# Gate k-steps between the attention's and the last heads' dependent matmuls, and x transposed earlier

## The chip, the cores and the metric

The program runs on one core of one Trainium2 chip. The metric is device time in microseconds of one launch, as the median of several runs; lower is better.

## The reference

One layer of a decoder trunk with eight sampled sequences of one new token each (NS = 8) beside one prompt of 1024 tokens (NP = 1024, NT = NP + NS = 1032 columns), at a model width of 1024, in float32:

```python
h  = rmsnorm(x) * (1 + scale1) + shift1              # shift, scale, gate from the conditioning c
z  = h @ w_in                                        # q|k|v, output gate, beta, decay, swa q|k|v, ga, gb
y_a = gated_rmsnorm(gated_delta_rule(conv4(q, k, v))) @ w_gdn_out       # 8 heads of 128 x 128
y_b = sliding_window_attention_with_sinks(q, k, v) @ w_swa_out          # 16 q heads, 4 kv heads, window 128
x  = x + gate1 * ((sigmoid(ga) * y_a + sigmoid(gb) * y_b) @ w_o)
h2 = rmsnorm(x) * (1 + scale2) + shift2
x  = x + gate2 * ((silu(dwconv3(h2 @ w_ffn_gate)) * (h2 @ w_ffn_up)) @ w_ffn_down)
return rmsnorm(x), and the new states (delta matrix, conv rows, window k and v, ffn conv rows)
```

## The kernel before

Activations lie transposed, features on partitions. A projection takes one column tile of 128 columns of `w_in` and runs over 8 slices of the contraction (k-steps) and three parts of the columns (384, 384 and 264 wide). Each k-step is a triple of matmuls, since an operand is split in a high and a low half: `mm3` (L168, L169, L170) adds high by high, low by high and high by low. The weights of a tile come by one transfer into a `raw` buffer (L132) and are split by ScalarE (L126) and VectorE (L127).

The stages of the first half are, in order: conditioning and modulation; `attention` of the prompt, four kv groups of 8 blocks, with the sampled sequences' own attention (`sample_softmax`) queued ahead of the last group's first block; eight DeltaNet heads; `branches` (the two output projections, and the sampled sequences' delta step). The FFN is the second half.

An attention block makes score products (L561, L562), a softmax on VectorE and ScalarE, transposes of the result (`pt`, L178) and value products (L598, L600).

A head runs five generators at once, which `weave` queues under different priorities. `unit_inverse` inverts a triangular matrix per chunk in rounds (matmuls L959 to L995). `head_projections` first projects this head's output gate (`sg`, one buffer, which is free again once the scan of the head before has read it for the last time at L904), and then q, k and v of head h + 2. `delta_scan` goes through the 8 chunks one after another: in each, L870, L873 and L877 depend on one another, with a VectorE or ScalarE step between them. `delta_prepare` makes head h + 1 ready: K and Q transposed back (`tp`, L178), their squares on ScalarE (L817), then K by K and Q by K (L835, L836), from which the next inverse starts.

`gates()` (L1186) is filler: 16 column tiles (the two branch gates, 8 tiles each), 16 x 3 x 8 = 384 k-steps, handed out one step at a time. A part ends with a tanh on ScalarE (L1198), an affine step on GpSimd and a store (L1200). Each tile's weights go into the place `fill_side`, which has one buffer each for the high half, the low half and the raw rows.

The order of instructions is that of a list scheduler: among those that a model of their times holds ready, the one of lowest priority number comes next. `later(f, by)` raises the number. `issue_after(ins)` pins what is queued under it behind one instruction. Each engine then runs its instructions strictly in that order. In a head the fillers have the number 10000, behind everything:

```python
streams = [(self.unit_inverse(pool, psum, h, prep[0]), 0, 1),
           (self.head_projections(pa, pool, h), 500, 100),
           (self.delta_scan(pool, psum, h, prep), 100, 1),
           (self.pieces(3), 10000, 100)]
```

`turn_rows` (L762) transposes x, nine row tiles, for the residual of the second half, and stores it; it runs in head 6. `last_rows` (L1019) transposes the last conv rows of the sequences and runs in head 7. All projections and fillers share two PSUM banks, pmm with two buffers and pmf with one.

Of the kernel before, what the change touches and what calls it, by code (L numbers as in the profile page):

```python
# [62 lines left out]
class Step:  # L63
    def __init__(self, ctx, tc, I, O):
# [12 lines left out]
        self.filler, self.ahead, self.fill_psum = iter(()), False, self.pmf  # L77

# [82 lines left out]

# [244 lines left out]
    def attention(self, pool, psum):  # L406
# [9 lines left out]
        self.filler, self.fill_where, self.gt = self.gates(), self.where, (pool, "vch")  # L416
# [115 lines left out]
    def attention_group(self, pool, psum, g, Q, KH, KL, V, sink):  # L532

        nc = self.nc
        for n0 in (0, 4):
# [14 lines left out]
    def attention_block(self, pool, psum, g, n, Q, KH, KL, V, sink, ob):  # L550
# [211 lines left out]
    def turn_rows(self, pa, pool):  # L762

        nc, I = self.nc, self.I
        self.xT = self.t(self.dr, [KC, P, NT], "xT")
        ys = [self.t(pool, [P, NCH, P], tag) for tag in "KQ"]
        for i, c in enumerate(range(0, NT, P)):
            w = min(P, NT - c)
            x, y = self.t(pa, [P, NT + 3], "z")[:, :NP], ys[i % 2]
            src = I["x_prompt"][0][c:c + P, :] if w == P else I["x_sample"].rearrange("b s d -> (b s) d")  # L770
            nc.sync.dma_start(x[:w], src)
            for k0 in (0, 4):
# [3 lines left out]
                nc.scalar.copy(y[:, k0:k0 + 4, :w], ps[:, :, :w])  # L776
            nc.sync.dma_start(self.xT[:, :, c:c + w].rearrange("k p n -> p k n"), y[:, :, :w])
            yield

    def delta_gate(self, pa, pool, h):  # L780
# [12 lines left out]
        self.sg = sg  # L793

# [60 lines left out]
    def delta_scan(self, pool, psum, h, prep):  # L855
# [3 lines left out]
        S = None  # L859
        so = self.t(pool, [P, NCH], "so", bufs=2)  # L860
        f = self.t(pool, [P, NCH], "f", bufs=2)
        for n in range(NCH):
# [4 lines left out]
            else:  # L867
                y = self.t(pool, [P, P], "y", bufs=2)
                ks = self.t(psum, [P, P], "rc", bufs=2)
                yield nc.tensor.matmul(ks, K[:, n, :], S, start=True, stop=True)  # L870
                nc.vector.scalar_tensor_tensor(y, ks, self.ned[:, h, n:n + 1], vn[:, n, :], op0=ALU.mult, op1=ALU.add)
            sp = self.t(psum, [P, P], "rc", bufs=2)
            yield nc.tensor.matmul(sp, W[:, n, :], y, start=True, stop=True)  # L873
# [3 lines left out]
            yield nc.tensor.matmul(ds, kd[:, n, :], s, start=True, stop=True)  # L877
# [10 lines left out]
            if n % 4 == 3:  # L888
# [10 lines left out]
                nc.vector.tensor_tensor(on, ops, bc(f[:, c0:c0 + 4], 2, P), op=ALU.mult)  # L899
# [285 lines left out]
    def gates(self):  # L1185
# [4 lines left out]
        load = lambda i: self.win(tiles[i][0], where=self.fill_where)  # L1190
# [17 lines left out]
    def branches(self, pool, pool2):  # L1208
# [3 lines left out]
        self.fill_where, self.gt, self.ahead, self.fill_psum = self.where, (pool, "sgx"), True, None  # L1212
# [3 lines left out]
        next(samples)  # L1216
# [538 lines left out]
    def run(self):  # L1755
        S, nc = ExitStack, self.nc
        self.constants()
        with S() as ca:
            with S() as c:
# [13 lines left out]
                self.attention(pool, psum)  # L1773
            pg = self.pool("pg", 1, ctx=ca)
            self.fill_side = pg, 1, 1
            self.fill_where, self.gt = self.fill_side, (pg, "gt")
            with S() as c:
# [6 lines left out]
                for h in range(H):  # L1784
                    prep = self.prep
# [12 lines left out]
        self.mm = [self.pmm, self.pmm, self.pmf]  # L1798
# [45 lines left out]
```

## Time and profile before

| what | value |
|---|---|
| median of the runs (least, most) | 2210.97 us (2206.25, 2214.44) |
| the profiled execution: time, span | 2216.06 us, 2214.3 us |
| TensorE busy | 2123.2 us, 96% of the span |
| VectorE, ScalarE, GpSimd busy | 1335.3, 801.2, 303.3 us |
| data moved | 228.16 MB, 103 GB/s over the span |
| attention's last group | about 377 to 428 us |
| the eight heads | about 458 to 1174 us |

Rows of a timeline give start, duration, engine, line, operation, output and inputs, and in brackets how long the engine sat idle before it and what released it. Rows of a table of windows give the window, its length, each engine's busy time with its count of instructions, and then TensorE's granted clock, the DMA share and GB/s. "Work" below is TensorE time at the full clock; a stretch loses its length less busy time by granted clock.

### The profile page before, as it was taken

To read this page: it belongs to the slowest core of one execution; us is meant where nothing else is said; L and a number is where in the kernel's file an instruction comes from. 1 tells how busy PE (TensorE), PEld (TensorE's weight loads), DVE (VectorE), ACT (ScalarE), POOL (GpSimd) and SP (SyncE) were. 2 spreads that over 40 slices of the span, in tenths; PEclk is the share of its full clock that TensorE was granted. 3 is DMA by queue.
4 is the path that set the end of the run, shared out by engine and by line. 5 is a ranking of instruction groups with operands and counts; after the bars stand their busy time and mean duration, and the time that the engine had idled before them with its cause. 6 is when DMAs were issued, how large, how long until landed. Compare 5 with 4: busy or idle time off the path is not lost.

```text
span 2214.3 us, 41267 instructions
## 1 busy us (share of the span) xinstructions
PE 2123.2 (96%) x16573; PEld 1995.0 (90%) x16573; DVE 1335.3 (60%) x2892; ACT 801.2 (36%) x2037; POOL 303.3 (14%) x395
## 2 busy tenths in 40 slices
PE   7998999899899999999978999999999999999998
PEld 3695788699899999999968899999999999999998
DVE  4556667574474664755423565468776776866565
ACT  3445445433333334234332032344343433421102
POOL 2000000022122121121110200002332332100000
PEclk8998999799999999999988999999999999999999
DMA  9411333232232231232753663612323222253202
GB/s 340 140 40 39 115 117 106 82 79 49 73 83 69 53 91 52 65 89 73 199 140 107 206 187 99 184 61 68 108 70 96 68 94 70 96 215 129 88 3 78
DMA packets 271346, 228.16 MB, mean 103 GB/s; under 512 B 57566, under 2 KB 237697, under 8 KB 271138
## 3 DMA queue, kind: packets, MB, share of 16 engines
q1 hardware_dynamic: 269826, 221.23, 32.5%
q10 hardware_dynamic: 1152, 3.70, 0.4%
q8 instruction: 130, 2.13, 0.4%
q14 instruction: 62, 0.51, 0.1%
q0 software_dynamic: 176, 0.59, 0.1%
HBM read 175.51 MB, written 52.35 MB: 103 GB/s over the span
## 4 chain that ended last, share of the span: by engine, by line
PE 84%; DVE 6%; DMA 5%; ACT 2%; issue 1%; SPq 1%; POOL 0%; DVEq 0%; POOLq 0%; ACTq 0%
PE mm L168 19%; PE mm L169 18%; PE mm L170 18%; PE wv L168 2%; PE wv L169 2%; PE wv L170 2%; PE wy L170 2%; PE wy L168 2%; PE wy L169 2%; PE pv L600 1%; PE mm L252 1%; PE pv L598 1%; PE pt L178 1%; PE tp L178 1%; PE sc L561 1%
## 5 line engine op out<-in xcount | busy, mean ns | idle before, releaser
L168 PE MATMUL mm<-b1h,wh 128*128 128x384 f32 (+1 forms) x1440 | 476.0, 332 | 9.6 <-DVE kx L496 4.5
L170 PE MATMUL mm<-b1h,wl 128*128 128x384 f32 (+1 forms) x1440 | 469.2, 327 | 3.9 <-DVE wl L127 3.9
L169 PE MATMUL mm<-b1l,wh 128*128 128x384 f32 (+1 forms) x1440 | 468.8, 326 | 0.1
L168 PEld LDWEIGHTS mm<-b1h,wh 128*128 128x128 f32 x1440 | 274.3, 191 | 22.1 <-issue 6.3
L169 PEld LDWEIGHTS mm<-b1l,wh 128*128 128x128 f32 x1440 | 274.6, 191 | 8.6 <-issue 7.0
L170 PEld LDWEIGHTS mm<-b1h,wl 128*128 128x128 f32 x1440 | 274.0, 190 | 6.6 <-DVE wl L127 4.7
L126 ACT ACTIVATE wh<-raw 128x1024 fp32r<-128x1024 f32 x77 | 80.7, 1048 | 156.4 <-PE mm L169 103.0
L168 PE MATMUL mm<-b2h,wh 128*128 128x384 f32 (+1 forms) x384 | 123.9, 324 | 1.6 <-DVE t L1220 1.0
L168 PE MATMUL mm<-pk,w 128*128 128x260 f32 (+1 forms) x440 | 124.4, 283 | 0.9 <-ACT pk L126 0.6
L169 PE MATMUL mm<-pk,w 128*128 128x260 f32 (+1 forms) x440 | 124.2, 282 | 0.8 <-DVE pk L127 0.8
L169 PE MATMUL mm<-b2l,wh 128*128 128x384 f32 (+1 forms) x384 | 123.5, 322 | 1.2 <-DVE b2l L127 1.2
L170 PE MATMUL mm<-pk,w 128*128 128x260 f32 (+1 forms) x440 | 124.2, 282 | 0.0
L170 PE MATMUL mm<-b2h,wl 128*128 128x384 f32 (+1 forms) x384 | 122.7, 321 | 0.0
L127 DVE TENSOR_TENSOR wl<-raw,wh 128x1024 fp32r<-128x1024 f32 x76 | 93.7, 1233 | 45.6 <-ACT wh L126 44.7
L170 PE MATMUL mm<-bmh,pk 128*128 128x256 f32 (+1 forms) x380 | 108.6, 286 | 0.8 <-DVE pk L127 0.8
L168 PE MATMUL mm<-bmh,pk 128*128 128x260 f32 (+1 forms) x380 | 108.7, 286 | 0.0
L1342 DVE SCALAR_TENSOR_TENSOR x<-mm,mT,x 128x256 f32<-128x256 f32 (+2 forms) x133 | 63.4, 481 | 72.7 <-PE mm L170 70.3
L169 PE MATMUL mm<-bml,pk 128*128 128x260 f32 (+1 forms) x353 | 100.6, 285 | 0.0
L170 PE MATMUL mm<-bmh,w 128*128 128x260 f32 (+1 forms) x320 | 91.7, 287 | 0.0
L168 PE MATMUL mm<-bmh,w 128*128 128x260 f32 (+1 forms) x320 | 91.6, 286 | 0.0
L127 DVE TENSOR_TENSOR w<-ws,w 128x512 fp32r<-128x512 f32 x88 | 60.2, 685 | 41.6 <-ACT w L126 41.6
L168 PEld LDWEIGHTS mm<-pk,w 128*128 128x128 f32 x440 | 82.7, 188 | 1.5 <-ACT pk L126 0.8
(578 smaller groups left out, 5727.8 us busy)
## 6 DMA issues: line engine op xcount, KB each, us to landing
raw<-in_w_in_dram SPq DMA_DIRECT2D x60, 512.0 KB
bml<-act SPq DMA_DIRECT2D x22, 516.0 KB
raw<-in_w_ffn_gate_dram SPq DMA_DIRECT2D x22, 512.0 KB
raw<-in_w_ffn_up_dram SPq DMA_DIRECT2D x22, 512.0 KB
raw<-in_w_ffn_down_dram SPq DMA_DIRECT2D x22, 512.0 KB
qst<-in_w_mod_dram SPq DMA_DIRECT2D x16, 512.0 KB
raw<-in_w_mod_dram SPq DMA_DIRECT2D x16, 512.0 KB
act<-fa SPq DMA_DIRECT2D x22, 260.0 KB
```

The lines of the kernel that those rows point to most:

```text
L126: self.nc.scalar.activation(hi, x, AF.Copy)
L127: (eng or self.nc.vector).tensor_tensor(lo, x, hi.bitcast(F32), op=ALU.subtract)
L168: mm(ps, whi, xhi, start=first, stop=False, **kw)
L169: mm(ps, whi, xlo, start=False, stop=False, **kw)
L170: mm(ps, wlo, xhi, start=False, stop=last, **kw)
L178: self.nc.tensor.transpose(out, in_, self.ident[:p, :p])
L252: nc.tensor.matmul(ps[32 * j:32 * j + 32], self.cT[:, k0 + j, :], ws[j // 2][:, j % 2, :], start=k0 == 0, stop=k0 > 0)
L561: nc.tensor.matmul(sc[:, r, 256 - w:256], q, KH[:, lo:lo + w], start=True, stop=False)
L598: nc.tensor.matmul(out, V[:, n, ch], pc[:, r::2, :], start=True, stop=n == 0)
L600: nc.tensor.matmul(out, V[:, n - 1, ch], pp[:, r::2, :], start=False, stop=True)
L1342: nc.vector.scalar_tensor_tensor(x[:, :np_], ps[:, :np_], self.mT[:, m + j, 8:9], x[:, :np_], op0=ALU.mult, op1=ALU.add)
```

## The change

- In the attention's last group, six gate k-steps follow every block, each pinned behind the block's last score product by `issue_after` and queued at `later(..., 120)`: 8 x 6 = 48 k-steps, two column tiles.
- In heads 6 and 7 the k-steps of gates are pinned behind the scan's matmuls, two k-steps (six matmuls) behind each, by `spaced()`. Four tiles are set in each of these two heads (`pieces(12)` and `pieces(24)`). There the gate steps alternate over three PSUM buffers and two weight places.
- The low-priority filler, `pieces(3)`, is left in heads 0 to 5 alone, which leaves six tiles for it. The output gate is now a stream of its own at 500, ahead of the projections at 600.
- `turn_rows` goes from head 6 to heads 1, 2 and 3, three row tiles in each, with a store for each half of a row tile. `last_rows` goes from head 7 to head 6.
- In the scan, the transposes of the first four chunks' output are issued after chunk 5 where they were issued after chunk 3.
- In `branches`, the sampled delta step is no longer begun ahead of the loop (its first `next` is gone).

The scheduler's order on TensorE is the same up to the attention's last group and from the branches' start on; its rows number 13399 before and 13397 after. In the changed kernel line numbers are higher by 10 to 21 (L168 is L178 there, L995 is L1016, L835 is L848, and the scan's L870, L873, L877 are L889, L892, L896).

```diff
-                self.mm3(ps, whi[:, k, :], wlo[:, k, :], xh[:, k, :], xl[:, k, :], k == 0, k == KC - 1)
+                with self.spaced():
+                    self.mm3(ps, whi[:, k, :], wlo[:, k, :], xh[:, k, :], xl[:, k, :], k == 0, k == KC - 1)
+
+    def spaced(self):
+
+        if not self.steps:
+            return nullcontext()
+        self.at += 1
+        i = min(self.at // self.every, len(self.steps))
+        return self.tc.issue_after(self.steps[i - 1]) if i else nullcontext()
...
                 self.attention_block(pool, psum, g, n, Q, KH, KL, V, sink[:, 4 * g:4 * g + 4], ob)
+                if g == 3:
+                    for _ in range(6):
+                        with self.tc.issue_after(self.scored.ins):
+                            self.later(lambda: next(self.filler), 120)
             for j in range(2):
                 nc.sync.dma_start(self.ob[2 * g + j][:, n0 * P:(n0 + 4) * P], ob[:, j])
             for _ in range((2, 1, 1, 1, 2, 1, 0, 0)[2 * g + n0 // 4]):
...
-                nc.tensor.matmul(sc[:, r, 256 - w:256], q, KH[:, lo:lo + w], start=True, stop=False)
+                self.scored = nc.tensor.matmul(sc[:, r, 256 - w:256], q, KH[:, lo:lo + w], start=True, stop=False)
...

     def head_projections(self, pa, pool, h):

-        self.delta_gate(pa, pool, h)
-        yield
         if h + 2 < H:
             yield from self.delta_project(pa, pool, h + 2)
-        if h + 1 == H:
-            for _ in range(8):
-                yield from self.pieces(3)
+        else:
+            yield from self.pieces(24 if h + 1 == H else 12)

     def pieces(self, n):
...
+    def turn_rows(self, pa, i0, i1):
         nc, I = self.nc, self.I
-        self.xT = self.t(self.dr, [KC, P, NT], "xT")
-        ys = [self.t(pool, [P, NCH, P], tag) for tag in "KQ"]
-        for i, c in enumerate(range(0, NT, P)):
+        if i0 == 0:
+            self.xT = self.t(self.dr, [KC, P, NT], "xT")
+        for c in range(i0 * P, i1 * P, P):
             w = min(P, NT - c)
-            x, y = self.t(pa, [P, NT + 3], "z")[:, :NP], ys[i % 2]
+            x = self.t(pa, [P, NT + 3], "z")[:, :NP]
             src = I["x_prompt"][0][c:c + P, :] if w == P else I["x_sample"].rearrange("b s d -> (b s) d")
             nc.sync.dma_start(x[:w], src)
             for k0 in (0, 4):
                 ps = self.t(self.pmm, [P, 4, P], "mm")
                 for k in range(4):
                     self.transpose(ps[:, k, :w], x[:w, (k0 + k) * P:(k0 + k + 1) * P])
-                nc.scalar.copy(y[:, k0:k0 + 4, :w], ps[:, :, :w])
-            nc.sync.dma_start(self.xT[:, :, c:c + w].rearrange("k p n -> p k n"), y[:, :, :w])
+                y = self.t(pa, [P, 512], "th", bufs=2).rearrange("p (k n) -> p k n", k=4)
+                nc.scalar.copy(y[:, :, :w], ps[:, :, :w])
+                nc.sync.dma_start(self.xT[k0:k0 + 4, :, c:c + w].rearrange("k p n -> p k n"), y[:, :, :w])
             yield
     def delta_gate(self, pa, pool, h):
...
+        self.steps, self.at, self.every = [], 0, 2
+        def step(ins):
+            if h + 2 >= H:
+                self.steps.append(ins.ins)
...
-                yield nc.tensor.matmul(ks, K[:, n, :], S, start=True, stop=True)
+                yield step(nc.tensor.matmul(ks, K[:, n, :], S, start=True, stop=True))
-            yield nc.tensor.matmul(sp, W[:, n, :], y, start=True, stop=True)
+            yield step(nc.tensor.matmul(sp, W[:, n, :], y, start=True, stop=True))
-            yield nc.tensor.matmul(ds, kd[:, n, :], s, start=True, stop=True)
+            yield step(nc.tensor.matmul(ds, kd[:, n, :], s, start=True, stop=True))
...
                 nc.vector.tensor_tensor(on, ops, bc(f[:, c0:c0 + 4], 2, P), op=ALU.mult)
+            if n in (5, NCH - 1):
+                c0 = 4 if n == NCH - 1 else 0
                 tp = self.t(psum, [P, 4, P], "rc", bufs=2)
                 for c in range(4):
-                    self.transpose(tp[:, c, :], on[:, c, :])
+                    self.transpose(tp[:, c, :], vn[:, c0 + c, :])
                 g = sg[:, c0 * P:(c0 + 4) * P]
                 nc.vector.scalar_tensor_tensor(g, tp.rearrange("p c i -> p (c i)"), self.onw, g,
                                                op0=ALU.mult, op1=ALU.mult)
...
-        load = lambda i: self.win(tiles[i][0], where=self.fill_where)
+        load = lambda i: self.win(tiles[i][0], where=self.fill_where[i % len(self.fill_where)])
...
-        self.fill_where, self.gt, self.ahead, self.fill_psum = self.where, (pool, "sgx"), True, None
+        self.fill_where, self.gt, self.ahead, self.fill_psum = [self.where], (pool, "sgx"), True, None
-        next(samples)
...
                     prep = self.prep
                     streams = [(self.unit_inverse(pool, psum, h, prep[0]), 0, 1),
-                               (self.head_projections(pa, pool, h), 500, 100),
+                               (self.delta_gate(pa, pool, h), 500, 1),
                                (self.delta_scan(pool, psum, h, prep), 100, 1),
-                               (self.pieces(3), 10000, 100)]
+                               (self.head_projections(pa, pool, h), 600, 100)]
+                    if h + 2 < H:
+                        streams.append((self.pieces(3), 10000, 100))
                     if h + 1 < H:
                         streams.append((self.delta_prepare(pool, psum, h + 1), 250, 1))
-                    else:
-                        streams.append((self.last_rows(pa), 1000, 0))
                     if h + 2 == H:
-                        streams.append((self.turn_rows(pa, pool), 700, 20))
+                        streams.append((self.last_rows(pa), 700, 50))
+                    if 0 < h < 4:
+                        streams.append((self.turn_rows(pa, 3 * h - 3, 3 * h), 800, 100))
                     self.weave(*streams)
+                    self.steps = []
             self.a2 = self.norm_scale("a2", 32, self.n2w)
-        self.mm = [self.pmm, self.pmm, self.pmf]
         with S() as c:
             pool2, pool = self.pool("p6b", 1, ctx=c), self.pool("p6", 1, ctx=c)
             self.branches(pool, pool2)
+        cg.close()
         self.wctx.close()
         self.second_half()

```

First place, TensorE in the attention's last group, behind the sampled softmax. `sc` are scores, `qst` and `kh`, `kl` the queries and keys, `pt` the transposed softmax, `pv` the values' products, `V` the values. Before:

```order
L561 MATMUL sc_3747<-kh_2531,qst_3196 128x256
L562 MATMUL sc_3747<-kl_2533,qst_3196 128x256
L561 MATMUL sc_3747<-kh_2531,qst_3197 128x256
L562 MATMUL sc_3747<-kl_2533,qst_3197 128x256
L178 MATMUL pt_3623<-ident,E_3590 128x128 x4
L561 MATMUL sc_3788<-kh_2531,qst_3100 128x256
L562 MATMUL sc_3788<-kl_2533,qst_3100 128x256
L561 MATMUL sc_3788<-kh_2531,qst_3101 128x256
```

After:

```order
L188 MATMUL mm_3412<-ident,pr_3407 128x128
L692 MATMUL mm_3416<-pT_3414,qst_3316 128x8 x4
L692 MATMUL mm_3416<-pT_3414,qst_3319 128x8 x4
L692 MATMUL mm_3416<-pT_3414,qst_3316 128x8 x4
L692 MATMUL mm_3416<-pT_3414,qst_3319 128x8 x4
L575 MATMUL sc_3842<-kh_2531,qst_3196 128x256
L576 MATMUL sc_3842<-kl_2533,qst_3196 128x256
L575 MATMUL sc_3842<-kh_2531,qst_3197 128x256
L576 MATMUL sc_3842<-kl_2533,qst_3197 128x256
L188 MATMUL pt_3696<-ident,E_3663 128x128 x4
L178 MATMUL mm_3502<-b1h_10_148,wh_3498 128x384
L179 MATMUL mm_3502<-b1l_11_149,wh_3498 128x384
```

The gate's triples (`mm` from `b1h`, `b1l` and `wh`, `wl`) now follow a block's score products and its transposes. They begin behind the last rows of `sample_softmax` (the `mm` from `pT`), which hold the same PSUM buffer; six blocks stand ahead of that row without gate work between them, where before all eight did.

Second place, TensorE at the change from head 4 to head 5, between the last step of one inverse (`tp` from `W` and `UZ`) and the next head's K by K. `tp` from `ident` are the K and Q transposes, `rc` and `o` the scan's products. Before, with `mm` the gate's triples:

```order
L168 MATMUL mm_11631<-b1h_12_150,wh_11598 128x384
L169 MATMUL mm_11631<-b1l_13_151,wh_11598 128x384
L170 MATMUL mm_11631<-b1h_12_150,wl_11599 128x384
L995 MATMUL tp_9477<-W_4141,UZ_9285 64x64 x8
L178 MATMUL tp_10112<-ident,K_8635 128x128 x4
L168 MATMUL mm_11660<-b1h_14_152,wh_11598 128x264
L169 MATMUL mm_11660<-b1l_15_153,wh_11598 128x264
L170 MATMUL mm_11660<-b1h_14_152,wl_11599 128x264
L168 MATMUL mm_11660<-b1h_14_152,wh_11598 128x264
```

After, the same place (the row behind the last one is the next head's first K by K):

```order
L1016 MATMUL tp_9829<-W_4332,UZ_9637 64x64 x8
L188 MATMUL tp_10464<-ident,K_9130 128x128 x4
L188 MATMUL rc_9122<-ident,vn_8605 128x128 x4
L892 MATMUL rc_9934<-vn_9603,W_4332 128x128
L188 MATMUL tp_10475<-ident,K_9130 128x128 x4
L896 MATMUL rc_9938<-s_9936,kd_9518 128x128
L900 MATMUL o_9933<-s_9936,A_9570 128x128
L188 MATMUL tp_10486<-ident,Q_9131 128x128 x4
L889 MATMUL rc_9944<-S_9941,K_8132 128x128
L899 MATMUL o_9933<-S_9941,Q_8133 128x128
L188 MATMUL tp_10496<-ident,Q_9131 128x128 x4
L892 MATMUL rc_9947<-y_9943,W_4332 128x128
```

Before, 50 to 74 gate matmuls stand in this place at each head change. After, at the changes 2 to 3, 3 to 4, 4 to 5 and 5 to 6, none do: between PE rows 3581 and 4784, which are heads 3 to 5, there is no gate work.

Third place, TensorE in head 7's scan, with `zl` the conv rows of `last_rows`. Before:

```order
L873 MATMUL rc_12091<-y_12087,W_4141 128x128
L877 MATMUL rc_12095<-s_12093,kd_10766 128x128
L881 MATMUL o_12063<-s_12093,A_10818 128x128
L870 MATMUL rc_12102<-S_12099,K_9579 128x128
L880 MATMUL o_12063<-S_12099,Q_9580 128x128
L873 MATMUL rc_12105<-y_12101,W_4141 128x128
L178 MATMUL mm_12333<-ident,zl 11x128 x4
L877 MATMUL rc_12109<-s_12107,kd_10766 128x128
L881 MATMUL o_12063<-s_12107,A_10818 128x128
```

After:

```order
L892 MATMUL rc_11894<-y_11890,W_4332 128x128
L178 MATMUL mm_12042<-b1h_12_150,wh_12009 128x384
L179 MATMUL mm_12042<-b1l_13_151,wh_12009 128x384
L180 MATMUL mm_12042<-b1h_12_150,wl_12010 128x384
L178 MATMUL mm_12042<-b1h_12_150,wh_12009 128x384
L179 MATMUL mm_12042<-b1l_13_151,wh_12009 128x384
L180 MATMUL mm_12042<-b1h_12_150,wl_12010 128x384
L896 MATMUL rc_11898<-s_11896,kd_11397 128x128
L900 MATMUL o_11866<-s_11896,A_11449 128x128
```

Two triples now stand between one scan matmul and the one that depends on it, and `last_rows` is gone from here.

More of the change, by code (lines that the diff above doesn't have):

```diff
@@ L77, in __init__ @@
         self.filler, self.ahead, self.fill_psum = iter(()), False, self.pmf
+        self.steps, self.at, self.every = [], 0, 1
     def pool(self, name, bufs, space=None, ctx=None, side=None):
@@ L415, in attention @@
         V = self.t(pool, [P, NCH, 256], "V", bufs=1)
-        self.filler, self.fill_where, self.gt = self.gates(), self.where, (pool, "vch")
+        self.filler, self.fill_where, self.gt = self.gates(), [self.where], (pool, "mrows")
         self.mods, self.mod_where = self.late_modulation(), (pool, (("wmh", 1), ("wml", 1), ("raw", 2), ("raw", 2)), "mrows")
@@ L793, in delta_gate @@
         self.sg = sg
+        yield
     def delta_prepare(self, pool, psum, h):
@@ L1773, in run @@
                 self.attention(pool, psum)
+            cg = S()
+            pgt = self.pool("pgt", 1, ctx=cg)
             pg = self.pool("pg", 1, ctx=ca)
             self.fill_side = pg, 1, 1
-            self.fill_where, self.gt = self.fill_side, (pg, "gt")
+            self.fill_where, self.gt = [self.fill_side], (pgt, "gt")
             with S() as c:
@@ L1784, in run @@
                 for h in range(H):
+                    if h + 2 == H:
+                        self.fill_where, self.fill_psum = [self.fill_side, self.where], None
+                        self.mm = [self.pmm, self.pmm, self.pmf]
                     prep = self.prep
                     streams = [(self.unit_inverse(pool, psum, h, prep[0]), 0, 1),
[L1787 removed]
+                               (self.delta_gate(pa, pool, h), 500, 1),
                                (self.delta_scan(pool, psum, h, prep), 100, 1),
[L1789 removed]
+                               (self.head_projections(pa, pool, h), 600, 100)]
+                    if h + 2 < H:
+                        streams.append((self.pieces(3), 10000, 100))
                     if h + 1 < H:
                         streams.append((self.delta_prepare(pool, psum, h + 1), 250, 1))
[L1792 to L1793 removed]
                     if h + 2 == H:
[L1795 removed]
+                        streams.append((self.last_rows(pa), 700, 50))
+                    if 0 < h < 4:
+                        streams.append((self.turn_rows(pa, 3 * h - 3, 3 * h), 800, 100))
                     self.weave(*streams)
+                    self.steps = []
             self.a2 = self.norm_scale("a2", 32, self.n2w)
[L1798 removed]
         with S() as c:
```

1 line of the change is left out of this document (removed).

## The prediction

> **What bounds the kernel now.** The page comes first: busy shares and the slices of the span.
>
> ```profile
> PE 2123.2 (96%) x16573; PEld 1995.0 (90%) x16573; DVE 1335.3 (60%) x2892; ACT 801.2 (36%) x2037; POOL 303.3 (14%) x395
> PE   7998999899899999999978999999999999999998
> ```
>
> TensorE is the bound nearly everywhere; only the slices around 400 and 1130 us are thin. The table of windows around the places that the change touches says what each stretch loses.
>
> ```profile
> 384.00:432.00 48.00, 38.07 (x175) 26.12 (x175) 27.47 (x101) 22.81 (x91) 1.41 (x4) 0.68 0.12 35
> 609.00:1072.00 463.00, 458.09 (x4029) 444.75 (x4028) 271.46 (x585) 174.68 (x515) 87.20 (x129) 1.00 0.27 75
> 1072.00:1088.00 16.00, 12.79 (x95) 12.42 (x93) 6.33 (x23) 6.80 (x18) 1.93 (x3) 1.00 1.04 278
> 1128.00:1184.00 56.00, 38.52 (x195) 32.39 (x194) 20.60 (x44) 19.14 (x47) 6.78 (x9) 0.70 0.67 195
> ```
>
> Length less busy time by granted clock is what a stretch loses: 48.0 - 38.07 x 0.68 = 22.1 us at the attention's end, 16.0 - 12.8 = 3.2 and 56.0 - 38.52 x 0.70 = 29.0 at the end of the last heads, but only 463.0 - 458.1 = 4.9 in the five heads between. TensorE's work stays the same, so the time moves by what these losses become. The kernel can gain at most 22 + 32 us; what it can lose lies in the 463 us that are full now because gates fill every hole.
>
> **The attention's end.** Rows of the timeline, TensorE's and one of VectorE's, from this stage and, the last five, from the heads:
>
> ```profile
> 375.83 0.60 PE L178 MATMUL mm<-ident,qst 128*128 128x128 f32 x4
> 381.09 0.66 PE L178 MATMUL mm<-ident,qst 128*128 128x128 f32 x4
> 392.72 4.87 PE L678 MATMUL mm<-pT,qst 128*128 128x8 f32 x32
> 397.63 2.82 DVE L682 COPY obs<-mm 64x8 f32<-64x8 f32 x16 [2.41 <-PE mm L678]
> 428.14 0.59 PE L168 MATMUL mm<-b1h,wh 128*128 128x264 f32 x1 [0.84 <-ACT z L718]
> 543.17 0.45 PE L170 MATMUL mm<-b1h,wl 128*128 128x384 f32 x1 [1.09 <-DVE wl L127]
> 785.81 0.28 PE L170 MATMUL mm<-b1h,wl 128*128 128x264 f32 x1
> 785.93 0.29 PE L168 MATMUL mm<-b1h,wh 128*128 128x264 f32 x1
> 871.04 0.34 PE L168 MATMUL mm<-b1h,wh 128*128 128x384 f32 x1
> 871.21 0.34 PE L169 MATMUL mm<-b1l,wh 128*128 128x384 f32 x1
> ```
>
> The 48 steps are 144 matmuls, about 22.4 us of work: the rows 871.04 and 871.21 are one 384-wide matmul apart (0.17), 785.81 and 785.93 one 264-wide (0.12), and a tile of 8 triples in three parts takes 8 x 3 x (0.17 + 0.17 + 0.12) = 11.0 to 11.2. They could fill a loss of 22. But in the new order they stand behind the sampled softmax, whose PSUM buffer they need, and that is a chain. Its rounds are 381.09 - 375.83 = 5.3 us apart; the last two of four and the rest run to the copies at 397.63 + 2.82 = 400.5, so 24.6 us, and with two more rounds and the softmax's other steps about 38. Beside it stand six bare blocks; I put that stretch at 42 us. It holds about 22.6 us of work (the window's 38.07 x 0.68 = 25.9 less two of its eight blocks, my estimate), so 19.4 are lost before the first gate. Two boundaries of gate tiles behind the single raw buffer cost about 2.5 us each: a wait such as the 1.09 at 543.17, with some microseconds of half clock behind it. That is 24.4 lost, where 22.1 in the window and some 2 to 3 just outside it are lost now. Term: 0. Bounds: -9 if the softmax's rounds run faster among bare blocks, +6 if all blocks are passed bare and the gates come behind them.
>
> **The last two heads.** Rows of the scan in head 7, at the full and at the half clock, and its ends:
>
> ```profile
> 1137.91 0.39 PE L877 MATMUL rc<-s,kd 128*128 128x128 f32 x2
> 1138.86 0.49 PE L870 MATMUL rc<-S,K 128*128 128x128 f32 x2
> 1147.32 1.03 PE L178 MATMUL mm<-ident,zl 128*11 128x128 f32 x4 [4.24 <-ACT th L1027]
> 1158.18 0.79 PE L870 MATMUL rc<-S,K 128*128 128x128 f32 x2
> 1161.91 0.79 PE L870 MATMUL rc<-S,K 128*128 128x128 f32 x2
> 1173.43 1.12 PE L178 MATMUL rc<-ident,vn 128*128 128x128 f32 x4 [3.97 <-DVE vn L899]
> 1176.26 0.69 PE L169 MATMUL mm<-b2l,wh 128*128 128x384 f32 x1 [1.17 <-DVE b2l L127]
> ```
>
> A chunk takes 1161.91 - 1158.18 = 3.7 us and one hop about 0.95 us (1138.86 - 1137.91). Two triples behind each hop are 6 matmuls, 4 x 0.17 + 2 x 0.12 = 0.92 us: the hop is just covered, the clock stays up, and a chunk takes 3 x (0.92 + 0.45) = 4.1 us, all of it work. The 4.24 of `last_rows` leaves this place, and the 3.97 before the last transposes is covered by the 2.2 tiles (25 us) that stand behind the scan. The loss of 32.2 becomes about 4. Term: -28, bounds -31 (nothing is left) and -22 (both weight places are late at their tile changes, four times 2.5 us).
>
> `turn_rows` and `last_rows` are the same matmuls elsewhere. Their x loads and the stores from `th` now pass through SP's queue in heads 1 to 3, where the queue is thin: 75 GB/s in the window of 463 us, against 278 at 1072.
>
> ```profile
> 1136.00:1144.00 8.00, 5.09 (x36) 3.74 (x34) 3.80 (x10) 2.87 (x7) 0.85 (x2) 1.00 1.19 301
> ```
>
> The states of `sample_delta` are now asked for behind the last gates. 4.2 MB at 301 GB/s is 14 us, and 147 rows of output projection, 25 us at 0.17, stand before their first use; term 0. GpSimd's affine steps are the same number; nothing waits behind them but their stores.
>
> **The head changes.** Here lies the price. At four head changes (2 to 3 up to 5 to 6) no gate stands any more. Rows of two changes of before, TensorE first, then ScalarE:
>
> ```profile
> 776.35 1.14 PE L995 MATMUL tp<-W,UZ 64*64 64x64 f32 x16
> 787.62 0.39 PE L835 MATMUL tp<-K 128*128 128x128 f32 x2
> 864.85 1.14 PE L995 MATMUL tp<-W,UZ 64*64 64x64 f32 x16 [1.61 <-ACT W L986]
> 865.92 1.11 PE L178 MATMUL tp<-ident,K 128*128 128x128 f32 x4
> 872.61 0.60 PE L178 MATMUL rc<-ident,vn 128*128 128x128 f32 x4
> 873.04 0.39 PE L873 MATMUL rc<-vn,W 128*128 128x128 f32 x2
> 878.06 0.38 PE L835 MATMUL tp<-K 128*128 128x128 f32 x2
> ...
> 781.78 0.37 ACT L875 ACTIVATE s<-rc,c 128x128 f32<-128x128 f32 x1 [2.09 <-PE rc L873]
> 782.28 0.28 ACT L817 ACTIVATE osq<-tp 128x128 f32<-128x128 f32 x1
> 782.68 0.28 ACT L817 ACTIVATE osq<-tp 128x128 f32<-128x128 f32 x1
> ```
>
> From the inverse's last step to the next head's first K by K it takes 787.62 - 776.35 = 11.3 and 878.06 - 864.85 = 13.2 us. Without gates, TensorE has 1.1 (L995), five bunches of four transposes at 0.43 (873.04 - 872.61) and about 0.5 for the scan, 3.8 us, to do in it. ScalarE's squares set the rest: 782.68 - 782.28 = 0.40 each, 16 of them 6.4; with L995 1.1, the first transposes 0.43, two scan copies of 0.37 and a little for the copy of L995's result, 9.3 us is the floor. I take 11.3, since the scan's squares (L892) share ScalarE: 7.5 lost. The inverse's rounds just ahead are bare too and lose a hop like the 1.61 at 864.85.
>
> The clock comes on top. Behind that 1.61 the four transposes at 865.92 took 1.11 where those at 872.61 took 0.60, and the windows show the granted clock:
>
> ```profile
> 864.00:868.00 4.00, 3.15 (x25) 2.99 (x26) 1.23 (x1) 3.85 (x14) 1.32 (x2) 0.74 0.07 20
> 868.00:872.00 4.00, 4.00 (x22) 4.00 (x21) 1.85 (x5) 3.02 (x17) 1.02 (x1) 0.83 0.59 165
> ```
>
> That is 3.15 x 0.26 + 4.0 x 0.17 = 1.5 us for one short wait; over a longer one I take 2. So 7.5 + 1.6 + 2 = 11 us for each change, 44 for four, less what is lost there now (4.9, and the clock's 1.5): +37. Bounds: at the floor, without the hop and the clock, 4 x 5.5 - 6.4 = +16, and at the 13.2 with everything 4 x 13 - 2 = +50; below even the floor, +8 if a projection of the next head slips into two of the four.
>
> On this the Trainium skill ("TensorE: Matmul & The Clock Gate", "Why this matters for your kernels") says that gaps of TensorE below about 3 us keep the full rate. By that rule the single waits here, each shorter than that, would cost no clock, and the sum would be 8 us lower; but the rows above show 0.74 and 0.83 behind a wait of 1.61.
>
> **The inverses.** From the last K by K to L959 the chain takes some 40 us:
>
> ```profile
> 540.32 0.39 PE L836 MATMUL tp<-Q,K 128*128 128x128 f32 x2
> 580.86 0.64 PE L959 MATMUL tp<-MR,U 32*32 32x32 f32 x52 [0.38 <-DVE MR L955]
> 1084.13 1.06 PE L178 MATMUL mm<-ident,z 128*128 128x128 f32 x8 [1.58 <-DMA z<-in_x_prompt_dram]
> ```
>
> In the new order 34 to 43 us of TensorE rows stand in that place in heads 2 to 7, so some heads run dry by a few microseconds, and the x rows bring waits on transfers like the 1.58. Term: +4, bounds 0 and +9.
>
> **The sum.** 0 - 28 + 37 + 4 = +13 us on a profiled execution of 2216.06, that is 2229; the median of the runs is 2210.97, 5 lower, so the prediction for the median is **2224 us**, 0.6% slower. About 0.5%, 11 us, is what a measurement of this kernel can tell from no change.
>
> **Rivals.**
>
> 1. Faster: the 11 to 13 us of a head change were made by the gates themselves. TensorE runs strictly in order, so each transpose waited behind some triples, and ScalarE stood idle for 2.09 before 781.78. If the bare chain shrinks to about 6 us (the squares start with the earlier tiles, and a projection moves up), a change costs 2 to 3 us with no clock drop, 10 for four, less 6.4: +4, and 0 - 28 + 4 + 2 = -22, or -17 with rounds that run dry: 2189 to 2194. It decides below 4 us a change. Against it: 16 squares of 0.40 are 6.4 by themselves. Chance 0.29.
> 2. No change: the chain is as long as forecast, but it is cut by short matmuls into waits of 1 to 2 us each, and the clock stays up through them as it did on the whole in the 463 us (granted 1.00, with 4.9 of waits in them). 8 of the 37 fall away: 0 - 28 + 29 + 4 = +5, 2216; with the chain nearer its floor 2205. Against it: the clock at 864. It is what the Trainium skill's rule above would give. Chance 0.26.
> 3. Slower by more: the gates behind the scan come too late for the branches, and loads of the states start only then and are not covered: 14 us on top, about 2238. For it: at 1136 the transfers already run at 301 GB/s. Against it: 25 us of cover. Chance 0.12.
> 4. The forecast, 2220 to 2232. Chance 0.33.
>
> **How the numbers follow.** Slower by over 0.5% (above 2222) are the forecast's and rival 3's cases less the forecast's lowest: 0.33 + 0.12 - 0.02 = 0.43. Within are rival 2 and that edge: 0.28. Faster (below 2200) is rival 1: 0.29. The range starts a little below rival 1's price, at 2188, which leaves out about 0.1 (both of the gains at their bounds). It ends at 2244, which takes in rival 3 at 2238 and the forecast with the head changes at their upper bound and the inverses at theirs (2224 + 13 + 5 = 2242); some 0.1 lies above.
>
> **What would show it.** Right: busy share in heads 3 to 5 down, with idle time of 7 us and a clock under 0.9 before L848 at four changes, released by ScalarE's squares; the 1128 to 1184 loss gone; gate steps in the attention only behind its last softmax row. Wrong: heads 3 to 5 still full (then rival 1), waits on the states' transfers at the first L1105 (rival 3), or a loss at the attention's end far from 22.

## The result, and the profile after

The changed kernel takes 2223.63 us (median of 10 runs, 2216.29 to 2226.18), the kernel before 2210.73 in the same comparison. The ratio is 1.0053, 95% interval 1.0038 to 1.0068: slower by 13 us, or 0.5%. The profiled execution took 2226.18 us, with a span of 2224.5.

One correction to the names used above. Counted from head 0, the four head changes without gate work are 3 to 4, 4 to 5, 5 to 6 and 6 to 7, one later than the text on the change and the prediction call them. The rows shown there are the right ones; the second place shown is the change from head 5 to head 6.

The page's first lines after, the busy shares and TensorE's slices:

```profile
PE 2121.5 (95%) x16573; PEld 2001.3 (90%) x16573; DVE 1338.6 (60%) x2892; ACT 801.9 (36%) x2037; POOL 297.7 (13%) x395
PE   7898998999899898999999999999999999999998
```

The thin slice near 1130 is gone. Between 450 and 1050 us three slices read 8 where one did before. For the stages, the table of windows: before, first the heads (from the first K by K to that of head 7), then the stretch from the end of the last inverse to the sampled delta step.

```profile
445.40:1053.00 607.60, 595.61 (x5266) 576.93 (x5265) 351.03 (x750) 225.78 (x664) 113.58 (x165) 0.99 0.26 71
1125.90:1198.00 72.10, 54.62 (x305) 48.17 (x305) 26.93 (x58) 20.79 (x49) 6.78 (x9) 0.76 0.58 169
```

The same two stretches after, then the attention's end after in two parts, and two of TensorE's rows in it:

```profile
465.70:1042.90 577.20, 542.06 (x4872) 521.17 (x4871) 342.54 (x744) 220.39 (x653) 93.82 (x145) 0.96 0.29 77
1121.20:1211.40 90.20, 85.19 (x536) 83.78 (x537) 28.68 (x58) 23.92 (x54) 12.95 (x19) 0.92 0.55 163
330.00:384.00 54.00, 43.56 (x236) 34.28 (x235) 36.48 (x117) 27.19 (x106) 1.53 (x3) 0.78 0.22 70
384.00:440.00 56.00, 55.55 (x355) 50.49 (x356) 23.75 (x48) 21.43 (x62) 4.59 (x8) 1.00 0.24 76
342.05 1.08 PE L188 MATMUL mm<-ident,qst 128*128 128x128 f32 x4 [3.23 <-DMA qst<-newd]
377.10 0.66 PE L178 MATMUL mm<-b1h,wh 128*128 128x384 f32 x1 [1.09 <-DVE obs L696]
```

TensorE's idle time in the heads went from 12.0 to 35.1 us and its clock from 0.99 to 0.96; at the end idle time went from 17.5 to 5.0. The attention's fill did not remove its loss but moved it: the first gate starts at 377.1, behind the last copy (`obs`) of the sampled softmax, the stretch from 384 to 440 is full, and the bare part now lies ahead of it. The clock of a long window is a rounded mean, so for the losses below (length less busy time by granted clock) I summed windows of 4 us:

| loss, us | before | after | difference | forecast |
|---|---|---|---|---|
| 330 us to the first K by K | 24.0 | 24.7 | +0.7 | 0 |
| heads, to head 7's K by K | 16.4 | 51.3 | +34.9 | +41 (37 and 4) |
| head 7's inverse | 3.2 | 0.8 | -2.4 | with the next row |
| from there to the sampled delta step | 28.4 | 11.1 | -17.3 | -28 |

That is +15.9 where the spans differ by 10.2; the stages that the change leaves alone lost less in this execution (37.2 against 41.6 from 4 to 330 us). One profile gives a stage's loss to no better than some 7 us: a kernel below whose heads are the same program lost 58.5 there.

### The profile page after: what moved, and what is told of

It is laid out like the page before. It is cut to its first block, busy times and chain, and to the rows that moved or that the text cites. A ratio compares the mean times of both kernels' runs of the same rounds, so it can differ in the third digit from the quotient of the medians.

```text
span 2224.5 us, 41297 instructions
## 1 busy us (share of the span) xinstructions
PE 2121.5 (95%) x16573; PEld 2001.3 (90%) x16573; DVE 1338.6 (60%) x2892; ACT 801.9 (36%) x2037; POOL 297.7 (13%) x395
## 3 DMA queue, kind: packets, MB, share of 16 engines
q8 instruction: 130, 2.13, 0.4%
## 5 line engine op out<-in xcount | busy, mean ns | idle before, releaser
L178 PE MATMUL mm<-b1h,wh 128*128 128x384 f32 (+1 forms) x1440 | 476.2, 332 | 11.1 <-DVE kx L506 4.5
L178 PEld LDWEIGHTS mm<-b1h,wh 128*128 128x128 f32 x1440 | 274.6, 191 | 22.8 <-issue 8.1
L178 PE MATMUL mm<-b2h,wh 128*128 128x384 f32 (+1 forms) x384 | 124.7, 326 | 2.7 <-DVE t L1240 2.4
L178 PE MATMUL mm<-pk,w 128*128 128x260 f32 (+1 forms) x440 | 124.4, 283 | 0.6 <-ACT pk L127 0.6
L178 PE MATMUL mm<-bmh,pk 128*128 128x260 f32 (+1 forms) x380 | 109.5, 288 | 0.0
L178 PE MATMUL mm<-bmh,w 128*128 128x260 f32 (+1 forms) x320 | 91.5, 286 | 0.0
L128 DVE TENSOR_TENSOR w<-ws,w 128x512 fp32r<-128x512 f32 x88 | 60.4, 687 | 41.6 <-ACT w L127 41.6
```

What stands on the lines that cost most here:

```text
L128: (eng or self.nc.vector).tensor_tensor(lo, x, hi.bitcast(F32), op=ALU.subtract)
L178: mm(ps, whi, xhi, start=first, stop=False, **kw)
```

## The experiments

Theory A: gate work is a stock of filler. Each tile taken out of the heads leaves holes bare there, in the inverse's rounds, at the changes and ahead of the inverse. Theory B: what was moved into the heads makes the waits. A ratio below is always to the kernel before.

**No gate steps in the attention.** Edit, of the changed kernel:

```diff
-                if g == 3:
-                    for _ in range(6):
-                        with self.tc.issue_after(self.scored.ins):
-                            self.later(lambda: next(self.filler), 120)
...
-                        streams.append((self.pieces(3), 10000, 100))
+                        streams.append((self.pieces(4), 10000, 100))
```

> The changed kernel without the 48 gate steps in the attention; their two tiles go back to the filler of heads 0 to 5 (four pieces a head for three). Theory A (the time lost in the heads is missing filler: the six tiles of filler are used up by head 3's inverse, and from there the inverse's rounds and the head changes are bare): the attention's end loses 24 us as in the other two kernels, the heads lose 38 in place of 51, and the time is about 2212. Theory B (what was moved into the heads, the rows of x and the new order of the streams, makes the waits there): the heads lose 51 as in the changed kernel, and since the two tiles of work come back without a hole to fill, the time is 2222 or more.

Measured 2213.38, ratio to before 0.9998 (0.9975 to 1.0020). The windows of the attention's end and of the heads:

```profile
330.00:440.60 110.60, 98.95 (x576) 82.23 (x575) 70.24 (x179) 54.07 (x196) 5.81 (x11) 0.86 0.31 95
440.60:1031.60 591.00, 564.92 (x5008) 543.42 (x5008) 346.42 (x742) 225.22 (x658) 102.50 (x151) 0.97 0.30 78
```

By slices the attention's end loses 24.5, the heads 44.2. The two tiles in the attention had bought nothing there, and were missing in the heads: that part of the change alone costs about 10 us, the whole slowdown within the error. The time is theory A's. The heads' 44.2 lies between the 38 of A and the 51 of B, and its distance from 51.3 is no more than one profile's error; for the stage, the table at the end of this section says more.

**Filler pinned to the inverses.**

```diff
+    def pinned(self, n):
+        self.steps, self.at, self.every = [self.first_round], 0, 1
+        yield from self.pieces(n)
+        self.steps = []
...
-                        streams.append((self.pieces(3), 10000, 100))
+                        streams.append((self.pinned(3), 10000, 100))
```

> The changed kernel with the three pieces (one tile) of filler of each head 0 to 5 pinned behind the first round of that head's inverse on TensorE, so that they can't be used up early. Theory A: the bare rounds and changes of heads 3 to 5 are filled, the heads lose 25 to 30 us in place of 51, time 2200 to 2208. Theory B: the waits stay, the heads lose 45 or more, time 2217 or more. In between, if what was filled ahead of the inverses of heads 1 and 2 comes back as a wait there: 2212.

Measured 2242.11, ratio 1.0132 (1.0100 to 1.0165): neither theory's number. The pin worked where it was put: over the eight heads the inverses' rounds lose 10.6 (23.4 in the changed kernel), and the changes 6.5 (11.4). But ahead of the inverses the loss is 53.0 in place of 17.7. The window from 8 us behind head 1's K by K up to its inverse, and a row in it:

```profile
560.90:596.80 35.90, 21.08 (x106) 16.92 (x106) 24.49 (x67) 8.49 (x27) 9.51 (x12) 0.66 0.30 68
574.00 0.80 PE L898 MATMUL rc<-y,W 128*128 128x128 f32 x2 [2.28 <-DVE y L896]
```

Here the gates had stood before they were pinned: from this K by K to the inverse the changed kernel has 2.5 tiles of triples, this one 0.7. The scan is bare, TensorE waits for its VectorE steps, and the clock falls to 0.66. Six tiles fill the holes from neither of the two places; the low priority had put them better than the pin.

**Rows of x in head 6 again.**

```diff
-                    if 0 < h < 4:
-                        streams.append((self.turn_rows(pa, 3 * h - 3, 3 * h), 800, 100))
+                    if h + 2 == H:
+                        streams.append((self.turn_rows(pa, 0, 9), 700, 20))
```

> The changed kernel with all nine row tiles of x transposed in head 6 again, as before (queued at 700). Theory A: the waits of 1.5 and 2.5 us on the loads of x in heads 1 to 3 go, two of 1.6 come back in head 6; time 2220 to 2226. Theory B: the heads lose 35 in place of 51, time 2208.

Measured 2229.47, ratio 1.0068 (1.0047 to 1.0089), a little above theory A's range; the heads lose 51.1. The waits on loads of x are gone and the loss ahead of the inverses falls from 17.7 to 8.9, but the changes and rounds lose as much more (44.4 for 34.8). That speaks against theory B as far as the rows of x go, and fits with the moved rows having been filler too. The other part of theory B, the new order of the streams, was not taken back in any run.

**Loads of the stored gates on GpSimd's queue.** In the changed kernel, VectorE and TensorE at the branches, and the transfers that SP issues ahead of them, in order (`sgx<-sgb` is a stored gate, `in_state_gdn_S` are the states):

```profile
1203.14 0.43 DVE L1240 TENSOR_TENSOR t<-mm,sgx 128x264 f32<-128x264 f32 x1 [9.89 <-DMA sgx<-sgb]
1203.62 0.49 PE L1164 MATMUL mm<-b1h,ones 128*128 128x128 f32 x2 [3.10 <-DVE t L1240]
1179.97 2.13 SPq L1284 DMA_DIRECT2D sgx<-sgb  x2
1182.77 0.38 SPq L1063 DMA_DIRECT2D b1h<-in_state_gdn_S_dram  x1
1183.46 0.90 SPq L1221 DMA_DIRECT2D sga<-gt  x1
1184.42 3.02 SPq L1063 DMA_DIRECT2D b1h<-in_state_gdn_S_dram  x2
1187.48 5.47 SPq L1063 DMA_DIRECT2D b1l<-in_state_gdn_S_dram  x3
1193.05 4.11 SPq L1063 DMA_DIRECT2D b1h<-in_state_gdn_S_dram  x2
1197.20 1.73 SPq L1284 DMA_DIRECT2D sgx<-sgb  x1
```

```diff
-        self.nc.sync.dma_start(s, src)
+        self.nc.gpsimd.dma_start(s, src)
```

> The changed kernel with the branches' loads of the stored gates on GpSimd's queue in place of SP's. If the wait of 3.1 us at 1203 comes from SP's queue, in which the third of these loads stands behind eight loads of states, that wait and some 3 us of half clock behind it go: time 2218. If the transfers themselves are late, since the states' loads hold the DMA engines at 300 GB/s, the wait stays: 2223.

Measured 2217.5, ratio 1.0019 (1.0001 to 1.0038). The same stretch, from the last inverse to the sampled delta step, and the first three of these loads, now on GpSimd:

```profile
1128.60:1218.80 90.20, 89.17 (x606) 87.33 (x607) 28.91 (x59) 24.57 (x55) 17.66 (x28) 0.98 0.55 165
1177.21 1.70 POOL L1284 DMA_DIRECT2D sgx<-sgb  x3 [0.89 <-DMA oa<-sg]
```

It loses 2.5 in place of 11.1. The wait was the order of SP's queue: the load of the third part stood behind eight loads of states and was issued 17 us after the first two. Issued together with them, it is no longer waited for. Of the 8.6 us between the two losses some 1.6 come from the clock at the scan's beginning (0.81 for 0.61 over 8.8 us), which the edit does not touch.

**The attention's gates in the other PSUM bank.**

```diff
+        self.fill_psum = self.pmm
```

(from the attention's start to its end)

> The changed kernel with the gate steps of the attention in the other PSUM bank (pmm in place of pmf, which the sampled softmax holds). They then stand between the softmax's rounds, from TensorE's row 1410 on, and not behind them. If the 24.7 us that the attention's end still loses are due to this wait for the bank: it loses 8 to 12, and the time is about 2210. If the stretch is bound by the softmax's chain on VectorE and ScalarE, or the weights come late behind the single raw buffer: it loses 20 or more, time 2220 to 2226.

Measured 2234.3, ratio 1.0086 (1.0065 to 1.0107), above all that was expected. The attention's end:

```profile
330.00:458.90 128.90, 121.75 (x780) 109.84 (x780) 73.19 (x168) 57.73 (x190) 8.55 (x16) 0.96 0.30 94
```

It loses 11.8: the bank was what kept the gates out, as expected. The heads were not as expected: they lose 69.5 in place of 51.3, and the rise lies ahead of the inverses of heads 3 to 5 (29.7 for 8.9), with waits of 0.9 to 2.5 us on the loads of x among them. The same six tiles stand elsewhere here: ahead of these three inverses the trace has 8.4 tiles of triples for the 10.4 of the changed kernel, and 2.1 at the three head changes that had none. Why the scheduler's order comes out so is not settled, but the place of the filler counts beside its amount.

**Ten tiles of filler, two in head 7.** (`pieces(5)` in heads 0 to 5, no attention steps, loads on GpSimd's queue.)

> No gate steps in the attention, five pieces a head in heads 0 to 5 (ten tiles of filler), four tiles in head 6, and the two that are left in head 7, where they are just the six matmuls behind each of the scan's steps; the stored gates' loads on GpSimd's queue. By the stock of filler the heads lost 51 us with six tiles and 44 with eight; with ten, theory A expects 30 to 36. The end of the scan in head 7 has no gates behind it and loses 4 to 8 more. Time 2198 to 2206. If the heads' loss doesn't depend on the stock (44 or more again): 2210 to 2216.

Measured 2212.83, ratio 0.9994 (0.9981 to 1.0007). The heads lose 25.4, less than forecast. So the time is that of the other case ("2210 to 2216") but not for its reason: the end loses 23.6 and not 4 to 8:

```profile
1145.00:1185.00 40.00, 22.39 (x126) 21.17 (x125) 16.94 (x29) 13.32 (x26) 8.61 (x12) 0.74 0.91 270
1155.98 1.12 PE L188 MATMUL rc<-ident,vn 128*128 128x128 f32 x4 [4.87 <-DVE vn L914]
1169.53 0.69 PE L178 MATMUL mm<-b2h,wh 128*128 128x384 f32 x1 [12.43 <-ACT b2h L127]
```

Behind the wait of 4.9 us for the scan's last output stands one of 12.4 us for the attention's output, `b2h`, which the branches load and split. In the changed kernel two tiles stand behind the scan's end; whether they had covered these waits is tried below.

**Eight tiles of filler beside the attention's two.** (`pieces(4)` on the changed kernel; head 7 again has two tiles.)

> The changed kernel with four pieces a head in heads 0 to 5 (eight tiles of filler), so that head 7 has two tiles and none behind its scan's end. Theory A: the heads lose 44 in place of 51, the end of head 7 loses 4 to 8 more than in the changed kernel: 2220 to 2225. If the tiles behind the scan's end covered nothing: 2214.

Measured 2230.57, ratio 1.0066 (1.0040 to 1.0092), above the 2220 to 2225 of theory A. The heads lose 47.0, the end 21.7: again the end without tiles behind the scan.

**The bank, eight tiles and the loads together.**

> The three edits together on the changed kernel: attention's gate steps in pmm, four pieces a head in heads 0 to 5, the stored gates' loads on GpSimd's queue. If the gains add up: 2223 - 13 - 2 - 6 = 2202; if the attention's loss isn't the bank's: 2215.

Measured 2221.32, ratio 1.0030 (1.0012 to 1.0047): neither the 2202 nor the 2215 of the forecast. The attention loses 8.2, the heads 39.6, the end 21.9. The bank's gain is whole here, and the uncovered end takes it back.

**Ten tiles of filler, two in head 6, four in head 7.**

```diff
-            yield from self.pieces(24 if h + 1 == H else 12)
+            yield from self.pieces(24 if h + 1 == H else 6)
```

> As the kernel with ten tiles of filler in heads 0 to 5 (and none in the attention, the stored gates' loads on GpSimd's queue), but head 6 gives two tiles and head 7 four, two of them behind its scan's end. If these two tiles cover the waits of 4.9 and 12.4 us that the last kernels show there, with the half clock behind them: the end loses 3 in place of 23.6, the inverse of head 7 loses some 10 for the two tiles that head 6 no longer has, time 2200 to 2205. If the waits only move behind the tiles: 2213 or more.

Measured 2194.73, ratio 0.9937 (0.9912 to 0.9961), from four runs: 0.6% faster than the kernel before, and below the forecast of 2200 to 2205. The heads, and from head 7's inverse past the sampled delta step:

```profile
439.70:1036.60 596.90, 578.23 (x5154) 556.85 (x5152) 349.69 (x745) 228.96 (x666) 109.51 (x157) 0.99 0.30 81
1120.00:1215.00 95.00, 94.68 (x652) 91.85 (x652) 29.87 (x59) 21.21 (x40) 17.70 (x28) 1.00 0.56 166
```

The end is full: the two tiles behind the scan's end do cover the waits. Head 7's inverse loses 3.0 and not some 10, against 0.8 in the kernel with four tiles in head 6: the two tiles behind head 6's last scan step had covered almost nothing.

**The bank, eight tiles, two in head 6, four in head 7.**

> Attention's two tiles in pmm, eight tiles of filler in heads 0 to 5, two in head 6, four in head 7, the loads on GpSimd's queue. The attention loses 8 to 12 as in the two kernels with this bank, the heads 40 to 47, head 7's inverse some 10, the end 3: 15 to 20 less attention loss than in the kernel with ten tiles, 15 to 20 more in the heads: 2200 to 2208. If the gain in the attention is given back in the heads altogether: 2213.

Measured 2204.93, ratio 0.9969 (0.9951 to 0.9987). Attention 11.7, heads 41.7, end 3.9, as forecast; head 7's inverse loses 5.7 for the forecast 10.

**Eight tiles, no attention steps, the loads on GpSimd's queue.**

> No gate steps in the attention, eight tiles of filler, four in head 6, four in head 7 (as in the first kernel of the study), and the loads on GpSimd's queue. The loads gave 6 us on the changed kernel; if that adds up: 2213 - 6 = 2207. If the wait on them was hidden by others: 2213.

Measured 2202.98, ratio 0.9965 (0.9949 to 0.9981), below the forecast 2207. Against the first experiment's 0.9998 the loads bring some 7 us; that adds up.

The stock of filler and the loss of the heads, over all kernels (gate tiles between the first K by K and head 7's):

| tiles | loss of the heads, us |
|---|---|
| 12.9 (before) | 16.4 |
| 10 | 25.4, 26.6 |
| 8 | 39.6, 40.5, 41.7, 44.2, 47.0 |
| 6 (after, and edits of it) | 51.1, 51.3, 58.5; pinned 69.1, with the other bank 69.5 |

From 13 tiles to 6 the loss rises with every step, by more in all than one profile's error; that is theory A. With the same six tiles it goes from 51 to 70, so the amount alone does not set it. The new order of the streams, the later transposes in the scan and the delta step's later start are in every one of these kernels but the first; what each of them is worth was not measured. In the kernel at 2194.73, which has them all, the heads lose 10 us more than in the kernel before; they can be part of that.

## Why the prediction was right, and where not

The median was forecast at 2224 and came at 2223.6. That the number is so close is luck: the direction and its reason (the gates are missing in the heads) were right, but the main term was worked out from the wrong holes, and the mis-sized terms fell out against each other.

*The attention's end, term 0*: measured +0.7, for the reason given. The gates wait for the softmax's bank, and the bare stretch ahead of them loses what the stage lost before; the experiment with the other bank shows the cause. Up to 384 us the loss is 54.00 - 43.56 x 0.78 = 20.0, for the forecast 19.4. A wait of 3.23 us on a transfer (at 342.05), which the sum did not have, is part of it. The 5 us for two tile boundaries did not come (0.4 are lost from 384 to 440), and some 4 us between 440 and the first K by K make up for them.

*The last two heads, term -28*: measured -2.4 and -17.3. The scan is covered as worked out. What was missed is SP's queue: the prediction cleared the states' transfers by their own first use, and did not count who is queued behind them. The load of a stored gate was, for 3.1 us and the half clock behind it, which is a smaller form of rival 3; moving it gave 6 us back. Of the 11.1 us that are still lost at the end, 11.40 - 7.08 x 0.70 = 6.4 lie there, from 1200 us on, and 8.80 - 8.13 x 0.61 = 3.8 at the scan's beginning (the windows are in the last section). The two tiles behind the scan's end covered far more than the 3.97 that the prediction gave them: without them the end loses some 20 us.

*The head changes, term +37*: the holes are there, but not where the sum had them. Rows of one bare change (from head 5 to head 6), windows of it, and the last one of an inverse's rounds:

```profile
950.59 1.11 PE L1012 MATMUL tp<-MR,UZ 64*64 64x64 f32 x16 [1.57 <-DVE MR L1009]
952.99 1.96 PE L1016 MATMUL tp<-W,UZ 64*64 64x64 f32 x16 [1.29 <-ACT UZ L1013]
960.57 0.66 PE L188 MATMUL tp<-ident,Q 128*128 128x128 f32 x4 [0.82 <-DVE kd L832]
961.45 0.49 PE L848 MATMUL tp<-K 128*128 128x128 f32 x2
961.03 0.28 ACT L830 ACTIVATE osq<-tp 128x128 f32<-128x128 f32 x1
962.75 0.28 ACT L830 ACTIVATE osq<-tp 128x128 f32<-128x128 f32 x1
952.99:961.45 8.46, 7.64 (x48) 6.96 (x48) 4.04 (x8) 5.29 (x27) 0.90 (x1) 0.68 0.16 63
948.00:952.00 4.00, 2.13 (x43) 1.79 (x36) 0.78 (x2) 3.76 (x15) 0.29 (x1) 0.95 0.07 20
952.00:956.00 4.00, 3.01 (x21) 2.90 (x22) 1.02 (x3) 1.49 (x4) 1.01 (x1) 0.50 0.01 2
956.00:960.00 4.00, 3.75 (x22) 3.37 (x21) 1.90 (x4) 3.38 (x18) 0.00 (x0) 0.69 0.32 131
960.00:964.00 4.00, 3.43 (x27) 3.24 (x28) 2.85 (x9) 2.93 (x17) 0.60 (x1) 1.00 0.00 0
853.90:878.90 25.00, 19.91 (x294) 17.89 (x293) 9.21 (x18) 9.64 (x29) 0.63 (x4) 0.86 0.34 91
```

From the inverse's last step to K by K it takes 961.45 - 952.99 = 8.5 us here, and 6.8, 7.6 and 9.1 at the other three, under the "floor" of 9.3. So the step that failed is "I take 11.3" with "7.5 lost". Before, gate triples ahead of the transposes had stretched the chain, as rival 1 said. The floor itself was too high, because K by K does not wait for all 16 squares: it takes one of the two `tp` buffers, which is free after the twelfth square (the row at 961.03), and the last square starts at 962.75, behind it. At all four bare changes twelve squares were done when K by K began. TensorE also had 5.1 to 5.6 us of work there (length less loss) and not 3.8. So it idles for 0.3 to 1.2 us, where 7 us, released by the squares, were to be the sign of being right.

The changes lose 11.4 in all against 3.4 before: +8, where the sum without its four hops of 1.6 us has +31. The inverses' rounds, for which the sum had those hops, 6.4, go from 3.4 to 22.7 in heads 0 to 6: +19. The window from 853.9 to 878.9 is one of them, 5.1 us idle at a clock of 0.86; one wait in it, of 1.43 us, is on a load of x. By its own test, below 4 us a change, rival 1 had the better account of the changes (1.2 to 3.5 us lost at each), though not of their clock, which was 0.64 to 0.78 at three of the four. Its time was wrong, since the rounds beside the changes were bare instead.

*The inverses, term +4*: in heads 0 to 6 the loss ahead of their first round goes from 9.7 to 17.6, +7.9. With +8 and +19 that is the +35 of the table, for a forecast of +41.

*The clock*: rival 2's price was wrong. In the rows above the granted clock is 0.50 from 952 to 956, and the longest single wait ahead of it is 1.57 us. The Trainium skill ("TensorE: Matmul & The Clock Gate", "Why this matters for your kernels") asks for no idle gaps above about 3 us so that the rate does not drop; in this stretch it dropped without one.

## What to carry to other kernels

Filler (independent work that the scheduler puts into holes) is a stock: before moving it into a visible hole, count the holes that it fills now, each with its length without the filler, and pay for all of them, not only the one that the trace names. Take it from where it covers least (here, behind head 6's scan), and find out what is late behind it before it is taken from the end of a stage. When loads are moved, look for the small load that now stands behind them in the same queue.

## What was not expected of the hardware

Between 948 and 952 us TensorE was busy for 2.13 of 4 us, with one wait of 1.57 us, the beginning of the one of 1.29, and only short matmuls around them, and from 952 to 956 the granted clock was 0.50. In the bare change of 8.46 us idle time is 8.46 - 7.64 = 0.8, and the loss 8.46 - 7.64 x 0.68 = 3.3: three quarters of it is the clock.

Still less was followed by a lower clock at the beginning of head 7's scan. The first row and window are the changed kernel's, then its window at the late gate load; the last two are the same place in the last experiment (eight tiles, no attention steps), whose waits there are the same:

```profile
1122.96 0.79 PE L892 MATMUL rc<-vn,W 128*128 128x128 f32 x2 [0.67 <-ACT W L1017]
1121.20:1130.00 8.80, 8.13 (x44) 7.99 (x45) 0.90 (x3) 0.95 (x2) 0.19 (x1) 0.61 0.20 60
1200.00:1211.40 11.40, 7.08 (x33) 6.27 (x32) 3.44 (x10) 1.06 (x1) 0.00 (x0) 0.70 0.71 211
1112.74 0.49 PE L888 MATMUL rc<-vn,W 128*128 128x128 f32 x2 [0.67 <-ACT W L1013]
1110.98:1119.78 8.80, 8.13 (x62) 8.00 (x63) 1.25 (x4) 1.80 (x4) 0.70 (x2) 1.00 0.20 60
```

Two waits of 0.67 us around short matmuls stand in both. The granted clock behind them is 0.61 in one execution and 1.00 in the other, so a price per wait cannot be read off one profile; this is part of why a stage's loss is known to no better than some 7 us.
